# Order of casts, jobs and the last bank in a two-layer DiT kernel on one core

## The chip, the cores and the metric

The kernel runs on one core of one Trainium2 chip. Measured is the device time of one execution, in microseconds (us); lower is better. The engines are TensorE (PE, matrix products into PSUM banks of 512 columns), VectorE (DVE), ScalarE (ACT), GpSimd (POOL) and SyncE (SP), which here only issues DMAs; DMAs are also issued from POOL's and ACT's queues. Every engine works through its own queue in order.

## The reference

Two layers of a diffusion transformer over 256 tokens of width 2048, with 256 context tokens and a branch width of 4096, all in float32. Each layer computes

```python
h = _rmsnorm(x, g) * (1 + scale) + shift      # scale, shift, gate: silu(c) @ ada_w + ada_b
y = branch(h)                                 # layer 0: Fourier, layer 1: attention
x = x + gate * (y @ w_out)

def _fourier_branch(h, w_in, w_mix):
    u, z = jnp.split(h @ w_in, 2, axis=-1)
    ug = u.reshape(b, n, FNET_GROUPS, FNET_GROUP_DIM)
    f = jnp.fft.fft2(ug, axes=(1, 3), norm='ortho').real
    f = jnp.einsum('bngc,gcd->bngd', f, w_mix).reshape(b, n, D_BRANCH)
    return f * jax.nn.silu(z)
```

The branch of layer 1 is windowed attention with a sink and the context keys, gated by `silu(z)` too. At the end stands one more `_rmsnorm` with the gain `fg`, whose result is stored.

## The kernel before

All products are float32 in three passes: an operand is split into a high part `h`, its rounding to the matmul format (a cast on ACT, L62), and a low part `l`, what is left (a subtraction on DVE, L63), and `mm3` (L74) sends the three products h·h, h·l and l·h into one PSUM bank. So every weight that arrives passes through ACT and DVE before PE can use it. Weights are loaded by SP into three rotating slots named `raw`; a load that reuses a slot waits until the split that reads it is done.

A tile framework allots buffers, puts in the semaphores and orders each engine's instructions by a cost model's due times; `tc.issue_after(x)` tells it to put what is issued inside behind `x` in the order, without a wait.

The stages, in order of time: the opening (to about 120 us); sixteen Fourier groups `g` (to about 325); the gate `z` of layer 0 in 32 blocks `b` of 48 matmuls (to about 677); the output projection of layer 0 in 32 steps `i` of 48 matmuls (to about 1031); the norm between the layers; keys, values and attention of layer 1 (to about 1690); its output projection with the final norm (to the end).

What the change touches:

- *Fourier group, L512 to 610.* The weights of a group come in two halves `kh`, each with two column sets whose sum (`p`) and difference (`m`) are wanted. `fold_uh` (L128) forms the difference `wm` on DVE (L130), and the sum of the first half on DVE too (L136); for the second half, an accumulating DMA on POOL's queue adds one set onto the other in HBM-to-slot direction (L139). `split_part` casts and subtracts (`wph`, `wpl`, `wmh`, `wml`). `load_m(g)` (L397 to 418) makes the group's mixing matrices: sums `mt` on DVE (L401, L402), their split `mh`, `ml`, matmuls, and from their banks `pqh` (ACT), `pql` (DVE) and `sp` (ACT L416, DVE L417). Before, the split of the second half's `p` is emitted ahead of `load_m(g)`:

```python
        elif g > 4:
            with tc.issue_after(evacs[g - 2][1]):
                f3 = [fold_uh(load_uh(g, kh), g, kh) for kh in range(2)]
            w = [split_uh(*f3[0]), {"m": split_part("m", f3[1][1])}]
            with after_evac(g - 1):
                w[1]["p"] = split_part("p", f3[1][0])
```

- *Matvec jobs.* `ada_jobs` (L624) multiplies the conditioning vectors `cb` into weights on DVE, 64 jobs of one 1 MB load (`in_adw`) each: jobs 0 to 31 and 40 to 55 have eight products (L639), jobs 32 to 39 and 56 to 63 four. `next(ada)` runs one job. The gate stage runs one per block from b=4; the output projection runs `ada_rate.get(i, 1)` in step `i` (L747).
- *Norm between the layers, L792 to 818.* `rsqrt` (L79) takes a power on POOL (L88) and one Newton step on DVE (L89 to L91). Its result `r4`, four columns, is split into `r4h` (L801) and `r4l`; eight matmuls (L815) spread it over the partitions into one bank, ACT copies that to `r_bc1` (L816), and the first activations of layer 1 are scaled by it (L851, L852).
- *The end, L1165 to 1243.* The last 512 output columns (`cb` = 3) of the two blocks of 128 tokens (`tb`) are summed over 32 steps `k`; those of `tb` = 1 from k = 20 on are `held`, twelve matmuls of 512 columns being the last four steps. `evac` multiplies a bank by the gate (L1172), adds the residual (L1173) and squares with a row sum (ACT, L1174); `finish(tb)` adds the row sums (L87), takes the root (L88 to L91), scales four column blocks on ACT and DVE, and stores each (L1214).

Of the kernel before, what the change touches and what calls it, by code (L numbers as in the profile page):

```python
# [16 lines left out]
P = 128  # L17
D = 2048
# [10 lines left out]
def tile_dit(ctx: ExitStack, tc: tile.TileContext, a: dict, out: bass.AP):  # L29
# [46 lines left out]
        PE.matmul(o, wh, xl, start=False, stop=False)  # L76
        return PE.matmul(o, wl, xh, start=False, stop=stop).ins  # L77

    def rsqrt(pool, src, w, tag, ahead=None):  # L79
        v = pool.tile([P, w], F32, tag=tag + "v", name=tag + "v")  # L80
        t = pool.tile([P, w], F32, tag=tag + "s", name=tag + "s")
        r = pool.tile([P, w], F32, tag=tag + "r", name=tag + "r")
        if ahead is None:
            V.tensor_scalar(v, src, 1.0 / D, EPS, op0=ALU.mult, op1=ALU.add)
        else:
            V.tensor_scalar(v, ahead, 1.0 / D, EPS, op0=ALU.mult, op1=ALU.add)
            V.scalar_tensor_tensor(v, src, 1.0 / D, v, op0=ALU.mult, op1=ALU.add).ins  # L87
        GP.tensor_tensor(r, v, mhalf[:, 0:w], op=ALU.pow)  # L88
        V.tensor_tensor(t, r, r, op=ALU.mult)  # L89
        V.scalar_tensor_tensor(t, t, -0.5, v, op0=ALU.mult, op1=ALU.mult)  # L90
        V.scalar_tensor_tensor(r, t, 1.5, r, op0=ALU.add, op1=ALU.mult)  # L91
        return r

# [67 lines left out]
    with tc.tile_pool(name="st", reuse_waits="tile", bufs=1, side="right") as st:  # L161
# [230 lines left out]

        ua = us.enter_context(tc.tile_pool(name="ua", reuse_waits="tile", bufs=2))

        def load_m(g):
# [12 lines left out]
            mm3(o[:, GD : 2 * GD], ch[:, 1, :], cl[:, 1, :], mh[:, 1, :], lr[:, 1, :], True, True)  # L408
            o2 = psum()
            PE.matmul(o2[0:96, 0:GD], ch[:, 3, 0:96], mh[:, 0, :], start=True, stop=False)  # L410
            PE.matmul(o2[0:96, 0:GD], ch[:, 3, 0:96], lr[:, 0, :], start=False, stop=True)
            pqh = ua.tile([P, 512], F32R, tag="pqh", name="pqh")
            pql = ua.tile([P, 512], F32R, tag="pql", name="pql")
            split(pqh, pql, o)
            sp = ua.tile([96, GD], F32R, tag="sp", name="sp")
            S.activation(sp, o2[0:96, 0:GD], AF.Copy, scale=mk[:, g : g + 1])  # L416
            V.scalar_tensor_tensor(sp[64:96, :], o2[64:96, 0:GD], mk[64:96, g : g + 1], sp[64:96, :].bitcast(F32), op0=ALU.mult, op1=ALU.subtract)  # L417
            return pqh, pql, sp

        for p in range(8, 12):  # L420
# [91 lines left out]
    for g in range(G):  # L512
        if g == 2:
            mix0 = ft_end[0]
        if g == 3:
            with tc.issue_after(f0_end[0]):
                f3 = [fold_uh(load_uh(g, kh), g, kh) for kh in range(2)]
            w = [split_uh(*f3[0]), {"m": split_part("m", f3[1][1])}]
            with tc.issue_after(ft_end[0]), tc.issue_after(ft_end[2]):
                w[1]["p"] = split_part("p", f3[1][0])  # L520
            mix1 = ft_end[0]
        elif g == 4:
            w = []
            for kh in range(2):
                with tc.issue_after((mix0, mix1)[kh]):
                    v, m = fold_uh(load_uh(g, kh), g, kh)
                    w.append({"m": split_part("m", m)})
                    with after_evac(g - 1) if kh else nullcontext():
                        w[kh]["p"] = split_part("p", v)
# [122 lines left out]
    with tc.tile_pool(name="yp", reuse_waits="tile", bufs=32) as ypool:  # L652
# [148 lines left out]
    V.tensor_copy(r4h, r4)  # L801
    V.tensor_tensor(r4l, r4, r4h.bitcast(F32), op=ALU.subtract)
    r_bc1 = act()
    with tc.issue_after(st_end[0]):
# [5 lines left out]
        for c, tb in ((0, 0), (0, 1), (1, 0), (1, 1), (2, 0)):  # L810
            x1_turn(tb, c)
    o = psum()
    for t in range(4):
        for i, rp in enumerate((r4h, r4l)):
            bc_end = PE.matmul(o[:, t * P : (t + 1) * P], rp[:, t : t + 1].broadcast_to([P, P]), identr, start=i == 0, stop=i == 1).ins  # L815
    S.copy(r_bc1, o)  # L816
    with tc.issue_after(bc_end):
        x1_turn(1, 2)
# [20 lines left out]
    with tc.tile_pool(name="h1", reuse_waits="tile", bufs=16) as h1p:  # L839
# [3 lines left out]
        with tc.tile_pool(name="kvp", reuse_waits="tile", bufs=2) as kvp:  # L843
            hc1 = []
            for k in range(KT):
# [2 lines left out]
                t = kvp.tile([P, 512], F32, tag="ht", name="ht")  # L848
                for s, h in ((0, hx), (1, hc)):
                    q = slice(s * N, (s + 1) * N)  # L850
                    V.scalar_tensor_tensor(t[:, q], x1[k][:, q], gs1[:, k, s : s + 1], r_bc1[:, q], op0=ALU.mult, op1=ALU.mult)  # L851
# [303 lines left out]
        with tc.tile_pool(name="fin", reuse_waits="tile", bufs=1) as fp:  # L1155
# [12 lines left out]
            def evac(tb, cb, o, c0=0, c1=512, col=None):  # L1168
# [3 lines left out]
                V.tensor_tensor(t, o[:, qx], gbc[:, q], op=ALU.mult)  # L1172
                V.tensor_tensor(x, x, t, op=ALU.add)  # L1173
                S.activation(t, x, AF.Square, accum_out=ss[:, col : col + 1])  # L1174
                if cb < 3:
                    GP.tensor_tensor(x, x, fg[:, q], op=ALU.mult)

# [18 lines left out]
                    evac(tb, 1 + c, o[tb][c])  # L1196
            o = [psum() for _ in range(2)]

            def step(k, tb, wh, wl, q=slice(0, 512)):
                mm3(o[tb][:, q], yh[k][:, tb * P : (tb + 1) * P], yh[k][:, N + tb * P : N + (tb + 1) * P], wh[:, q], wl[:, q], k == 0, k == NB - 1)  # L1200

            def finish(tb):
                s2 = fp.tile([P, 1], F32, tag="s2", name="s2", bufs=2)
                V.tensor_reduce(s2, ss[:, tb * 4 : tb * 4 + 3], axis=AX.X, op=ALU.add)
                r = rsqrt(fp, ss[:, tb * 4 + 3 : tb * 4 + 4], 1, f"f{tb}", s2)
                for c in (0, 3, 1, 2):
                    t = x2[tb][c]
                    if c == 3:
                        V.scalar_tensor_tensor(t, t, r, fg[:, c * 512 : (c + 1) * 512], op0=ALU.mult, op1=ALU.mult)
                    elif c == 2:  # L1210
                        V.tensor_scalar(t, t, r, None, op0=ALU.mult)
                    else:
                        S.activation(t, t, AF.Copy, scale=r)
                    (nc.scalar if tb and c == 1 else nc.sync).dma_start(out[tb * P : (tb + 1) * P, c * 512 : (c + 1) * 512], t)  # L1214

            held = []
            for kg in range(8):
# [128 lines left out]
```

## Time and profile before

| | us |
| --- | --- |
| three runs | 1856.7, 1855.9, 1852.46 (median 1855.9) |
| profiled execution, its own time | 1853.2 |
| its span in the trace | 1851.4 |
| PE busy | 1813.9 |
| DVE busy | 1390.3 |
| ACT busy | 956.9 |
| POOL busy | 172.6 |

The granted clock of TensorE in the profiled execution is 0.998 of full speed. In the rows of the profile, "A B ENGINE Lnn ..." stands for a start, a duration, an engine and a line of the kernel before; "out<-in" names the tiles, followed by the sizes (partitions x elements), and a bracket gives the idle time of the engine ahead of the instruction and what ended it. Matmuls are pipelined, so their durations overlap and the distance of starts is what one costs.

### The profile page before, as it was taken

Reading aid. Unit: us, or ns where it says so; the run is one execution under the profiler, and the core shown is the slowest. Engines: PE = TensorE matmul, PEld = TensorE weight load, DVE = VectorE, ACT = ScalarE, POOL = GpSimd, SP = SyncE. Lnnn points to the kernel's source line nnn. Section 1 sums busy time; section 2 is a strip of 40 time slices with the busy share of each in tenths; the row PEclk is TensorE's granted clock in tenths of the full one; section 3 lists DMA queues with packets and bytes.
Section 4 is the critical chain, followed back from the end, with each engine's and each line's share of the span. In section 5 each row is a group of like instructions: output and inputs, shape, how many; then the busy total and the mean of one; then the engine's idle time right before and its main releaser. Section 6 shows DMA issues by size and latency. Waiting matters only on the chain.

```text
span 1851.4 us, 26496 instructions
## 1 busy us (share of the span) xinstructions
PE 1813.9 (98%) x9905; PEld 1548.0 (84%) x9905; DVE 1390.3 (75%) x2773; ACT 956.9 (52%) x1660; POOL 172.6 (9%) x183
## 2 busy tenths in 40 slices
PE   6999999999999999999999999999999999999997
PEld 4689999888888888878888888888888888888886
DVE  5687889786868788578974836888878878887454
ACT  5444545532222242224322524888888888897343
POOL 0001112000000000000000001111220220300000
PEclk9999999999999999999999999999999999999999
DMA  9988889666656647654675324333333333444543
GB/s 394 418 309 223 234 226 257 230 224 228 233 202 250 229 167 273 239 216 158 227 283 211 114 91 152 123 135 129 123 116 135 132 119 137 160 138 182 183 180 137
DMA packets 74305, 366.37 MB, mean 198 GB/s; under 512 B 21121, under 2 KB 21265, under 8 KB 39105
## 3 DMA queue, kind: packets, MB, share of 16 engines
q1 hardware_dynamic: 50112, 326.67, 48.2%
q0 software_dynamic: 19920, 31.06, 6.6%
q10 hardware_dynamic: 4144, 6.95, 1.1%
q8 instruction: 78, 1.28, 0.3%
q14 instruction: 51, 0.41, 0.1%
HBM read 352.06 MB, written 12.59 MB: 197 GB/s over the span
## 4 chain that ended last, share of the span: by engine, by line
PE 85%; DMA 2%; DVE 2%; issue 2%; ACT 1%; POOL 0%; POOLq 0%; ACTq 0%; DVEq 0%
PE ps L75 22%; PE ps L76 22%; PE ps L77 22%; PE ps L1045 6%; PE ps L1047 3%; PE ps L1101 3%; PE ps L1116 2%; PE ps L1115 2%; PE ps L1081 2%; PE ps L1082 2%; DMA raw<-in_wu 1%; DMA raw<-in_adw 1%; PE ps L961 0%; DMA raw<-in_wo 0%; ACT wh L62 0%
## 5 line engine op out<-in xcount | busy, mean ns | idle before, releaser
L62 ACT CAST wh<-raw 128x1024 fp32r<-128x1024 f32 x333 | 349.5, 1051 | 541.9 <-PE ps L76 457.6
L63 DVE TENSOR_TENSOR wl<-raw,wh 128x1024 fp32r<-128x1024 f32 x333 | 421.2, 1267 | 231.7 <-ACT wh L62 228.5
L76 PE MATMUL ps<-act,wh 128*128 128x512 f32 x1024 | 398.4, 389 | 0.0
L75 PE MATMUL ps<-act,wh 128*128 128x512 f32 x1024 | 394.3, 389 | 1.2 <-ACT wh L62 1.2
L77 PE MATMUL ps<-act,wl 128*128 128x512 f32 x1024 | 392.8, 389 | 0.5 <-DVE wl L63 0.5
L75 PEld LDWEIGHTS ps<-act,wh 128*128 128x128 f32 x1024 | 192.3, 188 | 41.2 <-ACT wh L62 1.7
L77 PEld LDWEIGHTS ps<-act,wl 128*128 128x128 f32 x1024 | 192.3, 188 | 40.9 <-DVE wl L63 1.0
L76 PEld LDWEIGHTS ps<-act,wh 128*128 128x128 f32 x1024 | 192.3, 188 | 39.6
L639 DVE CUSTOM_DVE_ANT_0 raw<-raw,cb 128x512 f32<-128x512 f32 x256 | 172.4, 687 | 23.6 <-DMA raw<-in_adw 20.1
L1045 PE MATMUL ps<-h,wh 128*128 128x512 f32 x512 | 186.5, 399 | 0.0
L639 DVE CUSTOM_DVE_ANT_0 junk<-raw,cb 128x512 f32<-128x512 f32 x192 | 131.7, 686 | 24.2 <-DMA raw<-in_adw 13.1
L1047 PE MATMUL ps<-h,wl 128*128 128x256 f32 x512 | 138.3, 280 | 0.0
L76 PE MATMUL ps<-wl,h 128*128 128x512 f32 x320 | 125.4, 393 | 0.0
L77 PE MATMUL ps<-wh,h 128*128 128x512 f32 x320 | 124.3, 391 | 0.0
L75 PE MATMUL ps<-wh,h 128*128 128x512 f32 x320 | 123.7, 396 | 0.5 <-ACT h L852 0.5
L1045 PEld LDWEIGHTS ps<-h,wh 128*128 128x128 f32 x512 | 96.1, 188 | 18.4
L1083 DVE CUSTOM_DVE_ANT_0 ps<-ps,mask,nsink 128x512 f32<-128x512 f32 x128 | 92.1, 753 | 11.7 <-PE ps L1082 10.7
L1086 ACT ACTIVATE p<-ps,mx 128x512 f32<-128x512 f32 x128 | 87.3, 687 | 24.9 <-DVE mx L1083 24.3
L1047 PEld LDWEIGHTS ps<-h,wl 128*128 128x128 f32 x512 | 96.9, 189 | 1.4
L63 DVE TENSOR_TENSOR pl<-ps,ph 128x512 fp32r<-128x512 f32 x128 | 83.7, 684 | 9.9 <-ACT ph L62 9.1
L1091 ACT ACTIVATE p<-p,sm 128x512 f32<-128x512 f32 x128 | 85.4, 716 | 7.9 <-DVE sm L1089 7.9
L75 PE MATMUL ps<-act,wph 128*127 128x260 f32 x256 | 73.5, 287 | 1.1 <-DVE act L239 1.1
(329 smaller groups left out, 3572.0 us busy)
## 6 DMA issues: line engine op xcount, KB each, us to landing
raw<-in_wz SPq DMA_DIRECT2D x64, 1024.0 KB, 4.9
raw<-in_adw SPq DMA_DIRECT2D x64, 1024.0 KB, 4.9
raw<-in_awp SPq DMA_DIRECT2D x32, 1024.0 KB, 12.8
raw<-in_wo SPq DMA_DIRECT2D x32, 1024.0 KB, 6.3
raw<-in_wq SPq DMA_DIRECT2D x32, 1024.0 KB, 4.9
raw<-in_wu SPq DMA_DIRECT2D x32, 1016.0 KB, 7.9
raw<-in_wo1b SPq DMA_DIRECT2D x16, 1024.0 KB, 4.8
act<-in_xT POOLq DMA_DIRECT2D x32, 256.0 KB, 6.0
```

Of the source, the lines that this page charges most:

```text
L62: last_cast[0] = S.copy(h, src).ins
L63: last_sub[0] = V.tensor_tensor(l, src, h.bitcast(F32), op=ALU.subtract).ins
L75: PE.matmul(o, wh, xh, start=start, stop=False)
L76: PE.matmul(o, wh, xl, start=False, stop=False)
L77: return PE.matmul(o, wl, xh, start=False, stop=stop).ins
L639: V.tensor_tensor_reduce(junk if s == 0 and i < 3 else wf, wf, cb[:, s, kq * 512 : kq * 512 + 512], 1.0, 0.0, ALU.mult, ALU.add, acc[:, i, ...
L1045: PE.matmul(o[0], wh[:, q], hx1[k], start=k == 0, stop=k == KT - 1)
L1047: PE.matmul(o[0][:, 0:N], wl[:, q], hx1[k][:, 0:N], start=False, stop=False)
L1083: V.tensor_tensor_reduce(o, o, mask[:, tb, :], -0.125, nsink[:, i : i + 1], ALU.add, ALU.min, mx[:, tb : tb + 1])
L1086: S.activation(pt[:, tb, :], so[tb], AF.Exp, bias=mx[:, tb : tb + 1], scale=-1.0, accum_out=sm[:, tb : tb + 1])
L1091: S.activation(pt[:, tb, :], pt[:, tb, :], AF.Copy, scale=sm[:, tb : tb + 1])
L1101: PE.transpose(o[:, (kt * 2 + tb) * P : (kt * 2 + tb + 1) * P], pt[:, tb, c : c + P], ident)
```

## The change

Six edits, in the order of the kernel:

1. `rsqrt` can write its result a second time, into `high`; `r4h` is written so, ahead of `r4`, in place of the cast from `r4`.
2. In Fourier groups from 4 on, the split of the second half's `p` is emitted after `load_m(g)` and ordered behind its last instructions on ACT and DVE.
3. The 64 matvec jobs are dealt out in another way: two in the blocks b = 10, 17, 24 of the gate stage, and a new table for the output projection.
4. The eight spreading matmuls run over `r4h` for all four columns first, then over `r4l`.
5. The first scaling of layer 1 names the bank `r_ps` itself as its operand instead of the copy `r_bc1`.
6. At the end, the first 28 steps of the last bank are closed and evacuated without the square; the last four steps run in two new banks of 256 columns, each evacuated by itself. In `finish` the earlier row sums and the constant are added ahead on DVE, the last row sum on POOL; the stores go in the order `c` = 2 (first half), 0, 2 (second half), 3, 1.

```diff
@@ rsqrt
+        if high is not None:
+            V.scalar_tensor_tensor(high, t, 1.5, r, op0=ALU.add, op1=ALU.mult)
         V.scalar_tensor_tensor(r, t, 1.5, r, op0=ALU.add, op1=ALU.mult)
@@ load_m
-            S.activation(sp, o2[0:96, 0:GD], AF.Copy, scale=mk[:, g : g + 1])
-            V.scalar_tensor_tensor(sp[64:96, :], ...)
+            m_end[0] = S.activation(sp, o2[0:96, 0:GD], AF.Copy, scale=mk[:, g : g + 1]).ins
+            m_end[1] = V.scalar_tensor_tensor(sp[64:96, :], ...).ins
@@ for g in range(G)
             w = [split_uh(*f3[0]), {"m": split_part("m", f3[1][1])}]
-            with after_evac(g - 1):
-                w[1]["p"] = split_part("p", f3[1][0])
+            v = f3[1][0]
...
             pqh, pql, sp = load_m(g)
+        if g > 3:
+            with after_evac(g - 1), tc.issue_after(m_end[0]), tc.issue_after(m_end[1]):
+                w[1]["p"] = split_part("p", v)
@@ z_out
-                        next(ada)
+                        for _ in range(2 if b in (10, 17, 24) else 1):
+                            next(ada)
@@ output projection of layer 0
-        ada_rate = {2: 2, 5: 2, 8: 2, 11: 2, 15: 0, 16: 0, 19: 2, 22: 2, 25: 2, 28: 2, 30: 0, 31: 0}
+        ada_rate = {2: 2, 4: 2, 6: 2, 14: 0, 15: 0, 16: 0, 25: 2, 26: 2, 27: 2, 28: 2, 29: 0, 30: 0, 31: 0}
@@ norm between the layers
-    r4 = rsqrt(const, ssum[1], 4, "q", ssum[0])
-    V.tensor_copy(r4h, r4)
+    r4 = rsqrt(const, ssum[1], 4, "q", ssum[0], r4h)
...
-    for t in range(4):
-        for i, rp in enumerate((r4h, r4l)):
-            bc_end = PE.matmul(o[:, t * P : (t + 1) * P], rp[:, t : t + 1].broadcast_to([P, P]), identr, start=i == 0, stop=i == 1).ins
+    r_ps = o
+    for i, rp in enumerate((r4h, r4l)):
+        for t in range(4):
+            bc_end = PE.matmul(o[:, t * P : (t + 1) * P], rp[:, t : t + 1].broadcast_to([P, P]), identr, start=i == 0 and t == 0, stop=i == 1 and t == 3).ins
@@ first scaling of layer 1
-                    V.scalar_tensor_tensor(t[:, q], x1[k][:, q], gs1[:, k, s : s + 1], r_bc1[:, q], ...)
+                    V.scalar_tensor_tensor(t[:, q], x1[k][:, q], gs1[:, k, s : s + 1], (r_bc1 if k or s else r_ps)[:, q], ...)
@@ finish
-                V.tensor_reduce(s2, ss[:, tb * 4 : tb * 4 + 3], axis=AX.X, op=ALU.add)
-                r = rsqrt(fp, ss[:, tb * 4 + 3 : tb * 4 + 4], 1, f"f{tb}", s2)
-                for c in (0, 3, 1, 2):
+                n = 3 + tb
+                with tc.issue_after(sum_end[0]):
+                    V.tensor_reduce(s2, ss[:, tb * 4 : tb * 4 + n], axis=AX.X, op=ALU.add)
+                V.tensor_scalar(s2, s2, D * EPS, None, op0=ALU.add)
+                last = ss[:, tb * 4 + n : tb * 4 + n + 1]
+                GP.tensor_tensor(v, last, s2, op=ALU.add)
+                GP.tensor_tensor(r, v, mhalf[:, 0:1], op=ALU.pow)
+                V.tensor_tensor(t2, r, r, op=ALU.mult)
+                V.scalar_tensor_tensor(t2, t2, -0.5 * D**0.5, v, op0=ALU.mult, op1=ALU.mult)
+                V.scalar_tensor_tensor(r, t2, 1.5 * D**0.5, r, op0=ALU.add, op1=ALU.mult)
+                for c, c0, c1 in ((2, 0, 256), (0, 0, 512), (2, 256, 512), (3, 0, 512), (1, 0, 512)):
@@ last steps
-            for k, w in held:
-                step(k, 1, *w)
-            evac(1, 3, o[1])
+            for k, w in held[:-4]:
+                step(k, 1, *w, last=NB - 5)
+            evac(1, 3, o[1], square=False)
+            for h in range(2):
+                q = slice(h * 256, h * 256 + 256)
+                o[1] = psum()
+                for k, w in held[-4:]:
+                    step(k, 1, *w, q, NB - 4)
+                evac(1, 3, o[1], q.start, q.stop, 7 + h)
             finish(1)
```

More of the change, by code (lines that the diff above doesn't have):

```diff
@@ L77, in mm3, with rsqrt @@
         return PE.matmul(o, wl, xh, start=False, stop=stop).ins
-    def rsqrt(pool, src, w, tag, ahead=None):
+    def rsqrt(pool, src, w, tag, ahead=None, high=None):
         v = pool.tile([P, w], F32, tag=tag + "v", name=tag + "v")
@@ L393, in tile_dit @@
         ua = us.enter_context(tc.tile_pool(name="ua", reuse_waits="tile", bufs=2))
+        m_end = [None, None]
         def load_m(g):
@@ L527, in tile_dit @@
                     w.append({"m": split_part("m", m)})
-                    with after_evac(g - 1) if kh else nullcontext():
-                        w[kh]["p"] = split_part("p", v)
+                    if kh == 0:
+                        w[0]["p"] = split_part("p", v)
         elif g > 4:
@@ L850, in tile_dit @@
                     q = slice(s * N, (s + 1) * N)
-                    V.scalar_tensor_tensor(t[:, q], x1[k][:, q], gs1[:, k, s : s + 1], r_bc1[:, q], op0=ALU.mult, op1=ALU.mult)
+                    V.scalar_tensor_tensor(t[:, q], x1[k][:, q], gs1[:, k, s : s + 1], (r_bc1 if k or s else r_ps)[:, q], op0=ALU.mult, op1=ALU.mult)
                     a_ = S.activation(h[:, 0:N], t[:, q], AF.Identity, bias=sh1[:, k, s : s + 1]).ins
@@ L1166, in tile_dit, with evac @@
             ss = fp.tile([P, 9], F32, name="ss")
-            def evac(tb, cb, o, c0=0, c1=512, col=None):
+            sum_end = [None]
+            def evac(tb, cb, o, c0=0, c1=512, col=None, square=True):
                 col = tb * 4 + cb if col is None else col
@@ L1172, in evac @@
                 V.tensor_tensor(t, o[:, qx], gbc[:, q], op=ALU.mult)
-                V.tensor_tensor(x, x, t, op=ALU.add)
-                S.activation(t, x, AF.Square, accum_out=ss[:, col : col + 1])
+                sum_end[0] = V.tensor_tensor(x, x, t, op=ALU.add).ins
+                if square:
+                    S.activation(t, x, AF.Square, accum_out=ss[:, col : col + 1])
                 if cb < 3:
@@ L1197, in tile_dit, with step @@
             o = [psum() for _ in range(2)]
-            def step(k, tb, wh, wl, q=slice(0, 512)):
-                mm3(o[tb][:, q], yh[k][:, tb * P : (tb + 1) * P], yh[k][:, N + tb * P : N + (tb + 1) * P], wh[:, q], wl[:, q], k == 0, k == NB - 1)
+            def step(k, tb, wh, wl, q=slice(0, 512), first=0, last=NB - 1):
+                mm3(o[tb][:, q], yh[k][:, tb * P : (tb + 1) * P], yh[k][:, N + tb * P : N + (tb + 1) * P], wh[:, q], wl[:, q], k == first, k == last)
             def finish(tb):
-                s2 = fp.tile([P, 1], F32, tag="s2", name="s2", bufs=2)
-                V.tensor_reduce(s2, ss[:, tb * 4 : tb * 4 + 3], axis=AX.X, op=ALU.add)
-                r = rsqrt(fp, ss[:, tb * 4 + 3 : tb * 4 + 4], 1, f"f{tb}", s2)
-                for c in (0, 3, 1, 2):
-                    t = x2[tb][c]
+                s2, v, t2, r = (fp.tile([P, 1], F32, tag=n_, name=n_, bufs=2) for n_ in ("s2", "fv", "ft", "fr"))
+                n = 3 + tb
[9 more added lines that the diff above has]
+                for c, c0, c1 in ((2, 0, 256), (0, 0, 512), (2, 256, 512), (3, 0, 512), (1, 0, 512)):
+                    t = x2[tb][c][:, c0:c1]
+                    q = slice(c * 512 + c0, c * 512 + c1)
                     if c == 3:
-                        V.scalar_tensor_tensor(t, t, r, fg[:, c * 512 : (c + 1) * 512], op0=ALU.mult, op1=ALU.mult)
+                        V.scalar_tensor_tensor(t, t, r, fg[:, q], op0=ALU.mult, op1=ALU.mult)
                     elif c == 2:
@@ L1213, in finish @@
                         S.activation(t, t, AF.Copy, scale=r)
-                    (nc.scalar if tb and c == 1 else nc.sync).dma_start(out[tb * P : (tb + 1) * P, c * 512 : (c + 1) * 512], t)
+                    (nc.scalar if tb and c == 1 else nc.sync).dma_start(out[tb * P : (tb + 1) * P, q], t)
             held = []
```

2 lines of the change are left out of this document (1 added, 1 removed).

## The prediction

> **What bounds the kernel now.** I read the page's busy shares first, then the waits of TensorE by releaser, then the timeline around each wait that the change could touch.
>
> ```profile
> span 1851.4 us, 26496 instructions
> PE 1813.9 (98%) x9905; PEld 1548.0 (84%) x9905; DVE 1390.3 (75%) x2773; ACT 956.9 (52%) x1660; POOL 172.6 (9%) x183
> ```
>
> TensorE works for 1813.9 of 1851.4 us, so all idle time of PE together is 37.5 us. The change removes no matmul, so it can only win back some of that and shorten what follows the last matmul. The second view names the waits (columns: the waiting line and who released it; us in total, times, longest).
>
> ```profile
> PE ps L76 <- DVE ml L63: 2.4, 2, 2.2
> PE ps L75 <- ACT wh L62: 1.2, 1, 1.2
> PE ps L815 <- DVE r4h L801: 0.9, 1, 0.9
> ```
>
> These three are the ones that the edits stand next to: the Fourier groups (`ml`), one step of the output projection of layer 0 (`wh`), and the norm between the layers (`r4h`). Everything else that the edits can reach is the end after the last matmul. I go through them in this order.
>
> **Fourier groups.** Each group starts with `load_m`'s matmuls, whose first row has tile `mh,ch`.
>
> ```profile
> 163.23 0.28 PE L75 MATMUL ps<-mh,ch 128*128 128x256 f32 x1
> 177.67 0.27 PE L75 MATMUL ps<-mh,ch 128*128 128x256 f32 x1
> 194.52 0.27 PE L75 MATMUL ps<-mh,ch 128*128 128x256 f32 x1
> 159.90 1.48 POOL L139 DMA_DIRECT2D raw<-in_wu  x1 [11.90 <-DVE wm L130]
> 169.63 1.05 ACT L62 CAST wph<-raw 128x1016 fp32r<-128x1016 f32 x1 [5.83 <-DMA raw<-in_wu]
> 164.88 1.21 DVE L130 TENSOR_TENSOR wm<-raw 128x1016 f32<-128x1016 f32 x1
> 170.71 1.22 DVE L63 TENSOR_TENSOR wpl<-raw,wph 128x1016 fp32r<-128x1016 f32 x1 [4.62 <-ACT wph L62]
> 173.69 0.48 DVE L417 SCALAR_TENSOR_TENSOR sp<-ps,mk,sp 32x256 fp32r<-32x256 f32 x1
> 179.37 0.68 DVE L63 TENSOR_TENSOR ml<-mt,mh 128x512 fp32r<-128x512 f32 x1
> ```
>
> One group takes 177.67 − 163.23 = 14.44 us where nothing stalls; the next takes 194.52 − 177.67 = 16.85, so 2.4 us are lost in it, which agrees with the 2.4 of the wait for `ml`. Why `ml` is late is in the other rows. POOL issues the accumulating load at 159.90. ACT's cast `wph` needs it and starts at 169.63, after 5.83 us of idling; DVE idles 4.62 us behind the cast. The results of `load_m` (`pqh`, `sp` on ACT; `pql`, `sp` on DVE) stand behind that cast in both queues though they need nothing of it. So the fold of the next group and finally `ml` come at 179.37, when PE has already been asking for it for about 2.2 us.
>
> The change emits this split after `load_m` and orders it behind `m_end`. ACT then does `pqh` and `sp` while the load is in flight, and DVE, free at 164.88 + 1.21 = 166.1, goes on with the half fold (1.2), `pql` (0.7), `sp` (0.5), the fold `wm` (1.2), two `mt` (0.4 each), before it needs the cast. That is 4.4 us, to 170.5. The cast still starts at 169.63 and ends at 170.7; `wpl` and `wml` (1.2 each) bring DVE to 173.1, and `ml` (0.68) ends at 173.8. PE asks for it at 179.37 + 0.68 − 2.2 = 177.9, so it is some 4 us ahead, and a fold held up by its own load by up to that much still costs nothing. What is now later is the second half of `p`: `wpl` ends at up to 173.1 instead of 171.9. Its matmuls are the last quarter of the group that begins at 177.67, so it has over 10 us. Gain 2.4 (2.0 to 2.9).
>
> **Order of the matvec jobs.** The step of the output projection that lost time:
>
> ```profile
> 806.50 0.39 PE L76 MATMUL ps<-act,wh 128*128 128x512 f32 x1
> 806.73 0.39 PE L77 MATMUL ps<-act,wl 128*128 128x512 f32 x1
> 809.96 0.40 PE L75 MATMUL ps<-act,wh 128*128 128x512 f32 x1
> 799.01 1.22 DVE L63 TENSOR_TENSOR wl<-raw,wh 128x1024 fp32r<-128x1024 f32 x1
> 800.25 0.33 SPq L46 DMA_DIRECT2D raw<-in_wo  x1
> 807.26 1.99 ACT L62 CAST wh<-raw 128x1024 fp32r<-128x1024 f32 x2 [15.60 <-DMA raw<-in_wo]
> L639 DVE CUSTOM_DVE_ANT_0 raw<-raw,cb x256: 676/687/695, 371.0 to 985.5; 128x512 f32<-128x512 f32 x128
> raw<-in_adw SPq DMA_DIRECT2D x64, 1024.0 KB, 4.9
> raw<-in_wo SPq DMA_DIRECT2D x32, 1024.0 KB, 6.3
> 442.45 1.05 ACT L62 CAST wh<-raw 128x1024 fp32r<-128x1024 f32 x1 [3.90 <-PE ps L76]
> ```
>
> Undisturbed, matmuls start 806.73 − 806.50 = 0.23 us apart. From 806.73 to 809.96 lie 3.23 us for four of them, which take 0.92, so 2.3 are lost. The chain: at i=11 `ada_rate` puts two heavy jobs (eight products of 0.687 us, 5.5 us each) into one step. The step's second weight half gets its `wl` only at 799.01, behind five of those products; the load of the next weights reuses that slot and so leaves at 800.25, lands at 807.26, and PE is out of weights. In the new table i=7 to 13 have one job each; three heavy jobs have gone to the gate stage (b=10, 17, 24), the doubles at i=2, 4, 6 and 25 to 28 are light (four products, 2.75 us). Before i=12 DVE has one job (5.5 us) less ahead of it in that step, `wl` comes that much earlier and so does the load: 5.5 against a lateness of 2.3. Gain 2.3.
>
> What may come in its place. A gate step has 48 matmuls, at 0.23 us 11 us; DVE does two `wl` (2.4), one product with the gate (0.7, as 128x512 products take in the last fence) and one heavy job (5.5), 8.6 in all. A double makes it 14.1 and overruns the step by 3.1, caught up at 2.4 a step. Against that stands that the casts wait for PE to give up a weight buffer (3.90 us at 442.45), so a load may come about that much late, and a `wl` more, before PE sees it: cost 0 to 0.5 for each of three. Among the old doubles with two heavy jobs (i=2, 11, 19, 22) only one shows up in the waits. The four light doubles in a row at i=25 to 28 each ask of a slot: landing 4.9, own job 2.75, at worst the other job 2.75 and the two `wl` 2.4 in front, 12.8 against 11: 1.8 lost per step at the very worst, 7.2 over four, less the lead that the single jobs before them leave (one job and one landing fewer than the slot's step has room for, 11 − 4.9 − 2.75 = 3.4), so 3.8; at best 4.9 + 2.75 = 7.7, nothing lost. Cost taken 0, the lead being the likelier to do, range 0 to 3.8.
>
> **Norm between the layers.**
>
> ```profile
> 1033.72 0.16 DVE L91 SCALAR_TENSOR_TENSOR qr<-qs,qr 128x4 f32<-128x4 f32 x1
> 1033.92 0.17 DVE L801 CAST r4h<-qr 128x4 fp32r<-128x4 f32 x1
> 1034.23 0.30 PE L815 MATMUL ps<-act,r4h 128*128 128x128 f32 x1 [0.93 <-DVE r4h L801]
> 1035.43 0.58 ACT L816 COPY act<-ps 128x512 f32<-128x512 f32 x1 [1.29 <-PE ps L815]
> 1036.05 1.67 DVE L851 SCALAR_TENSOR_TENSOR ht<-act,gs 128x256 f32<-128x256 f32 x4 [1.77 <-ACT act L816]
> ```
>
> `r4h` is written in the place of 1033.72 instead of 1033.92, so PE starts 0.2 earlier. `r4l` keeps its time, 1034.12 + 0.16; the first matmul that needs it stands behind four on `r4h`, which start at 1034.03 and, at the 0.117 between narrow matmuls in the last fence, take till 1034.5: it is there. Gain 0.2. The first scaling (1036.05) would come 0.6 earlier if it read the bank beside ACT's copy. But in the built program it waits for that copy: both read one bank and are put one behind the other. So this edit is costed at 0 (−0.6 to +0.1). The Trainium skill, "PSUM — Partial Sum Buffer", section "PSUM bank collisions raise a hardware error ⚠️", speaks against it: two engines on one bank in the same partitions collide, two reads too, and a scheduler has to add a dependency. By that rule the edit gives 0, without it 0.6; no run so far shows which.
>
> **The end.**
>
> ```profile
> 1840.45 0.39 PE L77 MATMUL ps<-wh,ys 128*128 128x512 f32 x1
> 1840.88 0.69 DVE L1172 TENSOR_TENSOR act<-ps,gbc 128x512 f32<-128x512 f32 x1 [3.58 <-PE ps L77]
> 1842.33 0.63 ACT L1174 ACTIVATE act<-act 128x512 f32<-128x512 f32 x1 [4.78 <-DVE act L1173]
> 1843.08 0.16 DVE L87 SCALAR_TENSOR_TENSOR f1v<-ss,f1v 128x1 f32<-128x1 f32 x1 [0.79 <-ACT act L1174]
> 1843.32 0.55 POOL L88 TENSOR_TENSOR f1r<-f1v,mhalf 128x1 f32<-128x1 f32 x1 [7.78 <-DVE f1v L87]
> 1844.49 0.75 DVE L1209 SCALAR_TENSOR_TENSOR act<-act,f1r,fg 128x512 f32<-128x512 f32 x1
> 1845.15 0.48 DVE L1211 TENSOR_SCALAR act<-act,f1r 128x512 f32<-128x512 f32 x1
> 1845.23 1.30 SPq L1214 DMA_DIRECT2D out<-act  x3
> 161.50 0.41 DVE L603 TENSOR_TENSOR ft<-ps,gsb 128x256 f32<-128x256 f32 x1
> 255.80 0.28 PE L77 MATMUL ps<-act,wml 128*127 128x256 f32 x1
> 256.15 0.28 PE L77 MATMUL ps<-act,wml 128*127 128x256 f32 x1
> ```
>
> Matmuls: twelve of 512 columns at 0.23 (2.8 us) become 24 of 256 at (256.15 − 255.80)/3 = 0.117, 2.8 us: 0, at worst +0.1 for weights that load no faster than before. The sum of the first 28 steps is added beside them (two DVE steps, 1.4 us of 2.8), and so is the first bank's. On the path remains one bank of half the width: two DVE steps of 0.41 for 0.69 (−0.56), ACT's square shorter by about 0.2 of its 0.63. −0.76.
>
> The last sum moves from DVE (from 1843.08 to POOL's start at 1843.32, 0.24) to POOL, in front of the power. Its price there is not in the trace. The nearest row is that power, 0.55 for the same 128x1; below it nothing but a share of the hop. I take 0.45, so +0.2 (−0.1 to +0.4). [...]
>
> Stores: the first goes when ACT's scaling is done, 1845.23, 0.74 after the factor is used first (1844.49). In the new order the first is 256 columns of the DVE's scaling, some 0.28 of the 0.48 at 1845.15, so it leaves about 0.4 earlier. But four issues stand in SP's queue then instead of three, at (1.30/3) 0.43 each, the last behind `c=3`, about as late as before; and what is left, 1851.4 − 1845.23 = 6.2 us, is landing. So between −0.4 and +0.3; I take −0.15, as one of its two ends doesn't move. Sum of the end: 0 − 0.76 + 0.2 − 0.15 = −0.7 (−1.3 to +0.1).
>
> **The sum.** 2.4 + 2.3 + 0.2 + 0.7 = 5.6 us. The profiled execution took 1853.2 us, so it would take 1847.6. The three runs lie at 1852.46 to 1856.7 with a median of 1855.9; the middle of the four is (1853.2 + 1855.9)/2 = 1854.55, and 1854.55 − 5.6 = 1849.0 is the forecast. A difference of 0.2% (3.7 us) is about what a measurement of this kernel tells from none.
>
> **Rivals.**
> - *Stall put off, not removed.* The four light doubles at the end run out of their lead (2 to 3), or the second half of `p` is late, or the fold's own load holds `ml` (2.4). For it: the worst slot time, 12.8, exceeds the step. Against: the four jobs ahead of it are light, and the old light doubles show no wait. Gain 5.6 − 2.5 = 3.1, time 1851.4: no change that can be told. Chance 0.18.
> - *Gate stage becomes DVE's* (slower). In each of b=10, 17, 24 two heavy jobs in a step put the next `wl`, and the load that reuses its slot, behind 11 us of products. It decides once PE's lead is below the overrun of 3.1 and the landing does not overlap it; the price is then 3.1 and half a landing of 4.9, 5.6 each, 17 in all less the gain: +11, time 1866. For: the old i=11 did just this. Against: the 3.90 us for which the casts wait there, plus the weight halves already cast, and three of four such doubles cost nothing. Chance 0.07, and 0.03 more that something of the kind costs 10.
> - *The first scaling does read beside the copy.* Gain 6.2, time 1848.4. The wait in the built program speaks against it. Chance 0.05.
> - *The end gains nothing* (POOL's sum as dear as a power and small stores slower, +0.1 instead of −0.7): 4.8, time 1849.8; still the forecast's side. Chance 0.15.
> - *The forecast as summed*: 0.52.
>
> **The numbers.** The forecast, the third and the fourth rival are faster by over 0.2%: 0.72, less 0.03 for a spread of the runs that hides it; stall put off 0.18 and those 0.03 are no change, 0.21; slower 0.10. Low end: every term at its better end, 2.9 + 2.3 + 0.8 + 1.3 = 7.3, is 1847.3, and some 1.8 below for the spread of runs (4.2 from lowest to highest): 1845.5. High end: the stall put off at its dearest, 5.6 − 3.8 = 1.8 of gain, 1852.75, and 1.8 for the spread: 1854.5.
>
> **What would show it.** Right: no wait of PE for `ml`, nor for `wh` and `wl` of the layer-0 projection; `pqh` before `wph` on ACT; groups 14.5 us apart throughout; `r4h`'s wait 0.7; 2.2 us from the last matmul's evacuation to the sum shrunk to 1.4; a POOL sum of 0.3 to 0.5. Wrong: a new wait for `wl` or `wh` near 420 to 600 us or in i=25 to 29, a gain of the end under 0.3, or a first scaling that starts before ACT's copy is over.

## Result and the profile after

Five runs of the changed kernel lie at 1845.7 to 1846.4 us, median 1845.93; five runs of before at 1852.46 to 1856.7, median 1854.19. The ratio is 0.9957, with a 95% interval of 0.9944 to 0.9970. The forecast was 1849.0 in a range of 1845.5 to 1854.5: sign and range held, but the gain was 8.3 by medians where 5.6 was summed. The page of the changed kernel begins so:

```profile
span 1844.5 us, 26534 instructions
PE 1812.6 (98%) x9917; PEld 1548.5 (84%) x9917; DVE 1395.3 (76%) x2777; ACT 958.1 (52%) x1662; POOL 173.8 (9%) x185
```

Twelve more matmuls, no more PE time, 6.9 us less span. The profiled execution took 1846.4 where that of before took 1853.2, so the two traces hold 6.8 of the 8.3. In the waits of PE (us in total, times, longest) `ml`, `wh` and `wl` have no row any more, and two of the edited norm are left:

```profile
PE ps L822 <- DVE r4h L92: 0.7, 1, 0.7
PE ps L75 <- ACT h L859: 0.5, 1, 0.5
```

**Fourier groups.** The timeline of the changed kernel, first ACT, then DVE, at the place shown of before:

```profile
165.65 0.59 ACT L62 CAST pqh<-ps 128x512 fp32r<-128x512 f32 x1 [1.76 <-PE ps L77]
168.88 1.05 ACT L62 CAST wph<-raw 128x1016 fp32r<-128x1016 f32 x1 [2.28 <-issue]
```

```profile
165.50 1.22 DVE L138 TENSOR_TENSOR raw<-raw 128x1016 f32<-128x1016 f32 x1
166.64 0.69 DVE L63 TENSOR_TENSOR pql<-ps,pqh 128x512 fp32r<-128x512 f32 x1
167.36 0.48 DVE L421 SCALAR_TENSOR_TENSOR sp<-ps,mk,sp 32x256 fp32r<-32x256 f32 x1
169.97 1.22 DVE L63 TENSOR_TENSOR wpl<-raw,wph 128x1016 fp32r<-128x1016 f32 x1 [0.20 <-ACT wph L62]
171.10 1.21 DVE L63 TENSOR_TENSOR wml<-wm,wmh 128x1016 fp32r<-128x1016 f32 x1
172.23 0.69 DVE L63 TENSOR_TENSOR ml<-mt,mh 128x512 fp32r<-128x512 f32 x1
```

`pqh` is now ahead of `wph`, DVE works through the time in which it idled 4.62 us, and `ml` ends at 172.9 instead of 180.1. The prediction had 173.8.

**Norm.** The first scaling names the bank as its operand, and waits for ACT's copy of that bank nevertheless:

```profile
1029.78 0.59 ACT L823 COPY act<-ps 128x512 f32<-128x512 f32 x1 [1.07 <-PE ps L822]
1030.40 0.48 DVE L858 SCALAR_TENSOR_TENSOR ht<-act,gs,ps 128x256 f32<-128x256 f32 x1 [1.54 <-ACT act L823]
```

It starts 0.62 after the copy, as before (1035.43, 1036.05). This agrees with the Trainium skill, "PSUM — Partial Sum Buffer", section "PSUM bank collisions raise a hardware error ⚠️", by whose rule the edit was worth nothing.

**The end.**

```profile
1834.77 0.28 PE L77 MATMUL ps<-wh,ys 128*128 128x256 f32 x1
1835.08 0.43 DVE L1181 TENSOR_TENSOR act<-ps,gbc 128x256 f32<-128x256 f32 x1 [0.53 <-PE ps L77]
1836.00 0.42 ACT L1184 ACTIVATE act<-act 128x256 f32<-128x256 f32 x1 [0.90 <-DVE act L1182]
1836.33 0.19 ACT L1184 ACTIVATION_READ_ACCUMULATOR act<-act 128x1 f32 x1
1836.59 0.19 POOL L1219 TENSOR_TENSOR fv<-ss,s 128x1 f32<-128x1 f32 x1 [6.79 <-ACT act L1184]
1836.86 0.55 POOL L1220 TENSOR_TENSOR fr<-fv,mhalf 128x1 f32<-128x1 f32 x1
1838.03 0.62 DVE L1230 TENSOR_SCALAR act<-act,fr 128x256 f32<-128x256 f32 x2
1838.45 1.85 SPq L1233 DMA_DIRECT2D out<-act  x4
```

From the start of the last matmul to the end of the span pass 1844.5 − 1834.77 = 9.73 us, 10.95 before (1851.4 − 1840.45). 1.56 of them lie before ACT's read of its row sum (2.42 before), and 6.47 behind the first use of the factor (6.91 before). The last matmul is narrower now and starts later for the same work, so the fairer count is from DVE's first step behind it: 9.42 for 10.52 us (1835.08, 1840.88), 1.1 less. From the start of the sum on POOL to the power pass 0.27 us, where I took 0.45.

### The profile page after: what moved, and what is told of

Read it like the earlier page. It is cut to its first block, busy times and chain, and to the rows that moved or that the text cites. A ratio compares the mean times of both kernels' runs of the same rounds, so it can differ in the third digit from the quotient of the medians.

```text
span 1844.5 us, 26534 instructions
## 1 busy us (share of the span) xinstructions
PE 1812.6 (98%) x9917; PEld 1548.5 (84%) x9917; DVE 1395.3 (76%) x2777; ACT 958.1 (52%) x1662; POOL 173.8 (9%) x185
## 4 chain that ended last, share of the span: by engine, by line
PE 93%; DMA 3%; DVE 2%; ACT 1%; issue 1%; POOL 0%; POOLq 0%; SPq 0%; ACTq 0%; DVEq 0%
PE ps L75 24%; PE ps L76 24%; PE ps L77 24%; PE ps L1052 6%; PE ps L1054 3%; PE ps L1108 3%; DMA raw<-in_awp 2%; PE ps L1123 2%; PE ps L1122 2%; PE ps L1088 2%; PE ps L1089 2%; PE ps L213 1%; DMA raw<-in_wu 1%; PE ps L968 0%; DMA xn<-in_x 0%
```

## The experiments

The experiments were run in three series. All are compared with runs of the kernel before on the same chip. In the first series, the next four kernels, these had a median of 1854.13 us and a spread from 1850.8 to 1858.9.

**Edit 2 alone.** The diff is that of the Fourier groups, on the kernel before.

```diff
+        if g > 3:
+            with after_evac(g - 1), tc.issue_after(m_end[0]), tc.issue_after(m_end[1]):
+                w[1]["p"] = split_part("p", v)
```

> Only edit 2 (the split of the second half's p behind load_m) on the kernel before. Sum of parts: the waits for ml go and the span ends 2.4 to 3.1 us earlier, while the wait for wh and wl at i=12 (1.7) stays. Rival, the stall is only put off: under 1 us. Third theory, on the 1.4 us that the runs gained beyond the profiled executions: the runs of before spread over 4 us because one of the stalls differs from run to run, and the edit that removes it also removes the spread; if it is this one, its runs lie within 1 us of each other and the gain by medians is 3.5 to 4.5.

Median 1848.64 us (1847.06 to 1851.4), ratio 0.9974 [0.9962, 0.9985]: 4.8 us by the ratio, more than the 2.4 of the sum. The wait for `ml` is gone, and the wait at i=12 is there, smaller than the 1.24 and 0.53 of the profiled execution of before:

```profile
803.92 0.50 PE L75 MATMUL ps<-act,wh 128*128 128x512 f32 x1 [0.51 <-ACT wh L62]
805.17 0.50 PE L77 MATMUL ps<-act,wl 128*128 128x512 f32 x1 [0.52 <-DVE wl L63]
```

The runs still spread over 4.3 us, so the third theory does not hold in its simple form: not all of the spread goes with this stall.

**Edit 3 alone.**

```diff
-                        next(ada)
+                        for _ in range(2 if b in (10, 17, 24) else 1):
+                            next(ada)
...
+        ada_rate = {2: 2, 4: 2, 6: 2, 14: 0, 15: 0, 16: 0, 25: 2, 26: 2, 27: 2, 28: 2, 29: 0, 30: 0, 31: 0}
```

> Only edit 3 (the new deal of the matvec jobs) on the kernel before. Sum of parts: the wait at i=12 goes, the span ends 2.3 us earlier, the waits for ml (2.4) stay. Rival, the gate stage or the four light doubles stall: under 1 us, with a new wait for wh or wl. Third theory (spread): if the stall at i=12 is the one that differs from run to run, these runs lie within 1 us and the gain by medians is 3.5 to 4.5.

Median 1853.03 (1850.87 to 1859.66), ratio 1.0003 [0.9991, 1.0014]: no difference shown, where 2.3 us were summed. The interval reaches from 1.7 us faster to 2.6 us slower, so it excludes the 2.3 and not a smaller gain. The runs spread over 8.8 us, so the third theory fails for this stall as well. The trace has no wait for `wh` or `wl` and no new one, so the mechanism worked; the changed kernel with this edit undone, below, is a second measure of what it is worth.

**Edit 6 alone.** The diff is that of `finish` and the last steps.

> Only edit 6 (last four steps in two banks of 256 columns, sum on POOL, stores) on the kernel before. Sum of parts: 1.1 us from the start of the last matmul to the end as the trace of the changed kernel shows it (9.73 for 10.95, and 0.1 lost on PE), where the prediction had 0.7. Rival, the shorter end shows only in the trace: under 0.3. The spread of the runs stays at some 4 us.

Median 1852.36 (1849.65 to 1856.12), ratio 0.9990 [0.9981, 1.0000]: 1.9 us faster, give or take 1.8, in keeping with 1.1.

**Edits 1, 4 and 5 alone.**

> Edits 1, 4 and 5 (r4h ahead, order of the spreading matmuls, first scaling from the bank) on the kernel before. Sum of parts: 0.2 us, the wait for r4h falls from 0.9 to 0.7, and the first scaling still starts after ACT's copy is over. Rival, the scaling reads beside the copy: 0.8. Neither is told from none by the times; the trace decides. The spread of the runs stays at some 4 us.

Median 1853.76 (1851.99 to 1856.48), ratio 0.9995 [0.9986, 1.0005]: not told from none, as expected. The wait for `r4h` is 0.7.

These kernels give more than their times: with the first profiled execution, three of them are executions of the old Fourier order. The wait for `ml` in them, in the timeline of PE, for before, edit 3, edit 6 and edits 1, 4, 5 in this order:

```profile
180.11 0.38 PE L76 MATMUL ps<-ml,ch 128*128 128x256 f32 x1 [2.16 <-DVE ml L63]
```

```profile
180.76 0.56 PE L76 MATMUL ps<-ml,ch 128*128 128x256 f32 x1 [2.62 <-DVE ml L63]
```

```profile
179.08 0.39 PE L76 MATMUL ps<-ml,ch 128*128 128x256 f32 x1 [1.20 <-DVE ml L63]
```

```profile
181.54 0.58 PE L76 MATMUL ps<-ml,ch 128*128 128x256 f32 x1 [2.92 <-DVE ml L63]
```

The cast that stands behind the accumulating load started at 169.63 in the first of them, and in the other three as follows:

```profile
170.27 1.05 ACT L62 CAST wph<-raw 128x1016 fp32r<-128x1016 f32 x1 [6.28 <-DMA raw<-in_wu]
```

```profile
168.60 1.05 ACT L62 CAST wph<-raw 128x1016 fp32r<-128x1016 f32 x1 [4.87 <-DMA raw<-in_wu]
```

```profile
171.07 1.05 ACT L62 CAST wph<-raw 128x1016 fp32r<-128x1016 f32 x1 [6.37 <-issue]
```

From 168.60 to 171.07, 2.5 us, the cast comes later, and the matmul on `ml` comes 2.5 us later too (179.08, 181.54); PE waits only 1.7 us longer (1.20, 2.92), as it also arrives later. The lateness is handed on from the group before. The load ahead of this cast takes much the same in all four, 9.7 to 10.1 us from POOL's issue to the cast, but is issued between 158.92 and 161.18. The issue waits for DVE's `wm`, and DVE stands behind the same kind of cast one group earlier (150.30 to 152.57), whose own load took 10.4 to 12.3 us.

The wait is not the whole price. The first matmuls of this group and of the next, for edit 3 and for edits 1, 4 and 5:

```profile
177.86 0.28 PE L75 MATMUL ps<-mh,ch 128*128 128x256 f32 x1
196.67 0.28 PE L75 MATMUL ps<-mh,ch 128*128 128x256 f32 x1
```

```profile
178.23 0.39 PE L75 MATMUL ps<-mh,ch 128*128 128x256 f32 x1
197.37 0.28 PE L75 MATMUL ps<-mh,ch 128*128 128x256 f32 x1
```

The group takes 18.81 and 19.14 us here, 16.85 in the execution of before and 15.93 with edit 6, where an undisturbed one takes 14.44. So waits of 1.20, 2.16, 2.62 and 2.92 us cost 1.5, 2.4, 4.4 and 4.7: behind the two longest the granted clock of TensorE fell to half, as the last section shows. From the group that starts at 163 us to the last one, these four executions need 146.99 to 149.86 us and that of edit 2 alone 144.70 (163.30 to 308.00). So the old order costs 2.3 to 5.2 us there, 3.8 in the mean.

**The changed kernel again, and its old deal of jobs.** The second series had the changed kernel as a yardstick beside it, and one with edit 3 undone.

```diff
-        ada_rate = {2: 2, 4: 2, 6: 2, 14: 0, 15: 0, 16: 0, 25: 2, ...}
+        ada_rate = {2: 2, 5: 2, 8: 2, 11: 2, 15: 0, 16: 0, 19: 2, 22: 2, 25: 2, 28: 2, 30: 0, 31: 0}
```

> The changed kernel once more, on the chip on which the next three run, as their yardstick. If the width of its runs is a property of the kernel: 1845.5 to 1846.5 again, against 8 us for before. If it was the luck of one chip: a spread of 3 us or more.

> The changed kernel with the old deal of the matvec jobs. The stall at i=12 was 2.3 us in the profiled execution of before, 1.6 with edit 2 alone, 0.7 with edit 6 alone and absent with edits 1, 4 and 5 alone, so its size changes between executions. If it is the load's landing that makes it change: 0 to 2.5 us slower than the changed kernel, 1.2 in the median, and a spread of 2 us or more. If the stall was worth its 2.3 all the time: 2.3 slower with a spread as the changed kernel's.

The changed kernel: 1846.33 (1845.77 to 1848.08). With the old deal: 1846.67 (1845.72 to 1847.36), its fastest run as fast as the other's. The profiled execution of the latter shows a stall at i=12 and a span of 1845.4 against 1843.9; the medians differ by 0.3. So the double at i=11 costs between nothing and 2.3 us, by the execution, and 0.3 in these medians of five runs each. That the first spread of 0.7 us was a property of the kernel is not so: in the third series the changed kernel's runs went from 1845.77 to 1850.08.

**The sum on DVE.**

```diff
-                GP.tensor_tensor(v, last, s2, op=ALU.add)
+                V.tensor_tensor(v, last, s2, op=ALU.add)
```

> The changed kernel with the last sum on DVE instead of POOL. Before, from ACT's read of its row sum (1842.87) to the power (1843.32) were 0.45; after, with the sum on POOL, 0.53 (1836.33 to 1836.86). If these two rows tell it, this kernel is the same or 0.1 us faster, which only the trace can show. If the prediction's price held (0.2 for the sum on POOL), 0.2 faster. If the POOL's sum saves a hop, as the change would have it, 0.1 to 0.2 slower.

Median 1846.37 (1845.61 to 1849.51) against 1846.33. The trace decides:

```profile
1835.92 0.19 ACT L1184 ACTIVATION_READ_ACCUMULATOR act<-act 128x1 f32 x1
1836.13 0.16 DVE L1219 TENSOR_TENSOR fv<-ss,s 128x1 f32<-128x1 f32 x1 [0.32 <-ACT act L1184]
1836.37 0.55 POOL L1220 TENSOR_TENSOR fr<-fv,mhalf 128x1 f32<-128x1 f32 x1 [7.06 <-DVE fv L1219]
```

0.45 us from the read to the power, 0.53 with the sum on POOL: the move costs 0.08. An instruction of 0.19 on POOL, with the hop to it, takes a little longer than one of 0.16 on DVE with two hops. The power of 0.55, which I took as the nearest row, was a poor guide to it. The Trainium skill, "GPSIMD Engine Reference", section "3.1 Elementwise — side-by-side cycle accounting", has about 156 ns for the dispatch of an instruction in the column of DVE; POOL's has no figure, only that it takes two dispatch hops to DVE's one. The trace's 0.19 against 0.16 has POOL's instruction slower by 0.03, and so does not speak against that.

**The old order of the stores.**

```diff
-                for c, c0, c1 in ((2, 0, 256), (0, 0, 512), (2, 256, 512), (3, 0, 512), (1, 0, 512)):
+                for c, c0, c1 in ((0, 0, 512), (3, 0, 512), (1, 0, 512), (2, 0, 512)):
```

> The changed kernel with the old order and width of the stores (c = 0, 3, 1, 2, all of 512 columns). From the first use of the factor to the end of the span were 6.91 us before and 6.47 after. If the narrower first store makes that: 0.4 slower, 6.9 in the trace. If landing differs by itself between executions by that much: no change.

Median 1847.27 (1846.44 to 1849.86), 0.9 above the yardstick with overlapping runs. Its timeline:

```profile
span 1845.2 us, 26526 instructions
1838.32 1.33 ACT L1232 ACTIVATE act<-act,fr 128x512 f32<-128x512 f32 x2 [1.51 <-DVE fr L1223]
1839.07 1.31 SPq L1233 DMA_DIRECT2D out<-act  x3
```

6.88 us from the first use of the factor to the end, with the new order 6.47, and 6.91 before. The first store leaves 0.75 after the factor instead of 0.42. The difference is not the landing's own: from the first use of the factor to the end, all eight traces with the new stores have 6.37 to 6.49 us, all six with the old ones 6.84 to 6.91. So the new stores make 0.4 us. This run puts back order and width together, so it does not tell which of the two does it.

**The sum of the second half on DVE.** On the kernel before, order kept; the accumulating load is replaced by a DVE addition.

```diff
-        if kh == 0 and g > 2:
+        if g > 2:
             V.tensor_tensor(v[:, :, 0, :], v[:, :, 0, :], v[:, :, 1, :], op=ALU.add)
```

> The kernel before, its order of emission kept, with the sum of the second half of the Fourier weights formed by DVE (as that of the first half is) instead of by the accumulating load on POOL's queue. In four executions of the old order the cast wph at the head of ACT's queue started at 168.6, 169.6, 170.3 and 171.1 and PE then waited 1.2, 2.2, 2.7 and 3.1 for ml, one for one. If it is the landing of that load that the queue stands behind, PE no longer waits for ml there, the runs come to 1848 to 1850 as with edit 2 alone, less 1.2 us of DVE per group where DVE is short. If it is the order of the queue as such, whatever stands at its head, the wait stays at over 1 us.

Median 1849.36 (1848.37 to 1851.26), ratio 0.9979 [0.9970, 0.9988]. The wait for `ml` is gone although the order is the old one, and at the end of the last group a new wait stands:

```profile
PE ps L75 <- ACT mh L62: 1.3, 1, 1.3
```

So it was the load's landing behind which the queues stood. Taking the load away does nearly as much as passing it.

**Three heavy doubles in a row.**

```diff
-                        for _ in range(2 if b in (10, 17, 24) else 1):
+                        for _ in range(2 if b in (10, 11, 12) else 1):
```

> The changed kernel with its three heavy doubles of the gate stage in a row, b = 10, 11, 12 instead of 10, 17, 24. DVE then overruns by 3.1 us three times without a step to catch up, 9.3 in all. If PE's lead there is what the casts' waits for weight buffers showed, some 4 us and the halves already cast (5.4 each), a stall of 0 to 3 us with a wait for wl or wh near 430 to 470. If the lead is nil, as the slower rival had it, 9 us or more. If the lead covers it all: no difference to the changed kernel.

Median 1853.83 (1852.93 to 1856.43), 7.2 us above the yardstick of its series (1846.62). This lies between my bounds, and the test was not clean: the second vector `cb` is loaded after job 7, which falls into the doubles here, and DVE idles 4.33 us for it at 451.31. What follows is a stall of PE at the next weights:

```profile
470.75 0.50 PE L75 MATMUL ps<-act,wh 128*128 128x512 f32 x1 [3.37 <-ACT wh L62]
472.34 0.79 PE L77 MATMUL ps<-act,wl 128*128 128x512 f32 x1 [0.85 <-DVE wl L63]
```

The slower rival's mechanism exists, then; spread over b = 10, 17 and 24 it leaves no wait in the trace, presumably since each double finds its lead restored. How much lead there is was not measured.

**The scaling ahead of the copy.** On the changed kernel, with the sum on DVE.

```diff
-    S.copy(r_bc1, o)
...
-                    V.scalar_tensor_tensor(t[:, q], ..., (r_bc1 if k or s else r_ps)[:, q], ...)
+                    V.scalar_tensor_tensor(t[:, q], ..., (r_bc1 if k else r_ps)[:, q], ...)
+                    if k == 0 and s == 1:
+                        with tc.issue_after(a_end):
+                            S.copy(r_bc1, r_ps)
```

> The changed kernel with the first two scalings of layer 1 put ahead of ACT's copy of the same bank (the copy and the transposed stores behind the first activation), and the last sum on DVE. The trace of the changed kernel has the scaling start 0.62 after the copy (1029.78, 1030.40) and PE idle 0.5 before its first product. If the two readers of a bank are only put one behind the other, scaling first gives PE that 0.5; the sum on DVE gives 0.08: 0.5 to 0.6 faster, by the trace, and about as much by the medians. If the copy or the stores behind it are then late for the next product: 0 or slower.

> The changed kernel once more as the yardstick of this call: 1845.5 to 1846.5 in the median.

Medians 1846.05 (1845.0 to 1847.01) and 1846.62 (1845.77 to 1850.08): 0.6 in the expected direction, with overlapping runs. The timeline of the former:

```profile
1029.93 0.63 PE L822 MATMUL ps<-act,r4h 128*128 128x128 f32 x4 [0.73 <-DVE r4h L92]
1031.05 0.87 DVE L855 SCALAR_TENSOR_TENSOR ht<-act,gs,ps 128x256 f32<-128x256 f32 x2 [0.87 <-PE ps L822]
1032.13 0.50 PE L75 MATMUL ps<-wh,h 128*128 128x512 f32 x1
```

From the first spreading matmul to the first product of layer 1 pass 2.20 us, and PE no longer waits for `h`; in the changed kernel it was 2.87 (1028.60 to 1031.47). So 0.67 us are won there, in this trace. The profiled execution as a whole is slower than the yardstick's (spans 1845.2 and 1844.0), because a wait of 1.3 us for `ml` came up in a later Fourier group. DVE's rows ahead of it:

```profile
274.05 1.22 DVE L63 TENSOR_TENSOR wpl<-raw,wph 128x1016 fp32r<-128x1016 f32 x1 [2.33 <-ACT wph L62]
275.19 1.21 DVE L132 TENSOR_TENSOR wm<-raw 128x1016 f32<-128x1016 f32 x1
```

Edit 2 orders the split behind `load_m`, but not behind the next fold `wm`; in this group the fold, and with it `mt` and `ml`, still stands behind the split that waits for the late cast. As the faster version this kernel is likely, not shown by its times.

## Why the prediction was right, and where its sizes were off

**Fourier groups: right in mechanism, too small in size.** The step "gain 2.4 (2.0 to 2.9)" read the price of the stall from one execution. At the first place alone it was 1.5, 2.4, 4.4 and 4.7 us in four executions, because the load came between 0 and 2.5 us later and because the clock fell behind the longer waits; the prediction had neither. Edit 2 alone brought 4.8 us by the ratio (2.8 to 7.0), and the 3.8 of the four traces lies within that. That the untraced runs are like the traced ones is likely, since the edit touches nothing else, but not shown. The two figures of 2.4 that the prediction found in agreement are not the same time: the row of waits holds 2.16 in this group and 0.26 in the next, and the next lost 0.6 more (209.53 − 194.52 = 15.01), which the sum left out.

The 4 us of slack worked out for `ml` were 177.9 − 172.9 = 5.0 at this place in the changed kernel's trace. It is not as much everywhere: two later groups of that trace take 14.89 and 14.70 us, so the sign "groups 14.5 us apart throughout" was missed there, and the executions with three doubles in a row and with the scaling first had 0.8 and 1.3 us of this wait in later groups.

**Jobs: right in mechanism, too large in size.** The step "5.5 against a lateness of 2.3. Gain 2.3" took the dearest execution for all of them. The stall was 2.3 there, 1.6 with edit 2 alone, 0.8 with edit 6 alone, absent with edits 1, 4 and 5 alone, 1.5 in the changed kernel with the old deal and 1.3 with the sum of the second half on DVE, 1.25 in the mean of the six. Edit 3 alone made no difference that the runs show, and undone in the changed kernel it costs 0.3 in the median; neither excludes 1.25. This error and that of the Fourier groups have opposite signs, and both come from reading a price in one execution; that they partly cancel in the medians is luck.

**What may come in its place: right.** No wait for weights arose, neither in the gate stage nor behind the four light doubles. "Cost taken 0" held at both. One double was misread: that of i=6 is not light, as its second job is job 40, with eight products. No wait followed it either.

**Norm: right.** 0.2 for `r4h`; 0 for the scaling from the bank, for the reason given. Scaling first, which the change did not do, shows that the 0.6 were there to be had.

**The end: too small.** Predicted 0 − 0.76 + 0.2 − 0.15 = −0.7. By the trace, from DVE's first step behind the last matmul to ACT's read of the row sum −0.74 (1.99 to 1.25), the sum on POOL +0.08, the stores −0.44, together −1.1. The new matmuls cost nothing: the two traces lie 5.8 us apart ahead of them and 5.8 at that first step (1840.88, 1835.08). The mis-sized terms are the sum on POOL and, above all, the stores: I let the last issue decide, but the end came earlier with an earlier first issue, though SP's last issue ended 0.2 later behind the factor.

**The sum.** 5.6 was worked out for the profiled execution, which gained 6.8. Of the difference of 1.2, 0.7 lie in the Fourier groups (the last of them ends 3.1 us earlier, at 322.95 for 326.01, where I had 2.4: the shorter waits of 0.2 and 0.3 in later groups went too), 0.4 at the end and 0.1 elsewhere. Of the further 1.5 to the 8.3 of the medians, 1.0 is by how much the median of before lies above its profiled execution (1854.19, 1853.2), and 0.5 by how much the median of the changed kernel lies below its own (1845.93, 1846.4). The measured 1845.93 lies below 1847.3, the sum of all terms at their better ends; the range holds it only by the 1.8 that was added for the spread of the runs.

## What to carry to other kernels

A stall behind a transfer has no price, only a distribution: before it is put into a sum, look at how late that load is in several executions and at the granted clock behind the stall, and keep the range open on the side of the later landing. An instruction that waits for a slow load at the head of a queue stops everything behind it on that engine and on those that it feeds; move what is ready ahead of it first, and only then look for time elsewhere. Naming a PSUM bank instead of its copy as an operand brings nothing as long as the copy is first in order; put the reader on the critical path first.

## What the runs showed of the hardware

Behind a long enough idle time of TensorE its granted clock fell to half for about 3 us. The view of busy time by stretch (stretch; us; busy time of PE, PEld, DVE, ACT, POOL; granted clock; DMA share; GB/s) has, behind the wait for `ml` of 2.16 us before, of 2.62 us with edit 3 and of 2.92 us with edits 1, 4 and 5, in this order:

```profile
182.00:184.00 2.00, 2.00 (x19) 2.00 (x18) 1.34 (x2) 0.00 (x0) 0.00 (x0) 1.00 1.09 312
```

```profile
182.00:184.00 2.00, 2.00 (x11) 2.00 (x11) 1.99 (x3) 0.00 (x0) 0.44 (x1) 0.50 1.18 363
```

```profile
182.00:184.00 2.00, 2.00 (x11) 2.00 (x11) 2.00 (x4) 0.51 (x3) 0.54 (x1) 0.50 1.35 303
```

In the kernel with three doubles in a row, around and behind the stall of 3.37 us:

```profile
466.00:470.70 4.70, 1.38 (x7) 0.80 (x5) 4.63 (x16) 1.64 (x3) 0.00 (x0) 1.00 0.70 263
473.00:475.50 2.50, 2.50 (x8) 1.98 (x7) 2.46 (x8) 0.00 (x0) 0.00 (x0) 0.54 1.02 383
475.50:480.00 4.50, 4.50 (x22) 3.70 (x21) 3.67 (x11) 1.64 (x2) 0.00 (x0) 1.00 0.79 275
```

The clock fell behind idle times of 2.62, 2.92 and 3.37 us, in the last case only in a second wait of 0.85 us that came right behind, and stayed at 1.00 behind those of 1.20 and 2.16. The Trainium skill, "TensorE: Matmul & The Clock Gate", "Part 1: The HAM clock gate", has the clock drop after an idle window of about 3.4 us; in this kernel it fell behind shorter ones, and the measurement decides. Whether there is a fixed limit, and where between 2.16 and 2.62 us, no run here shows. So a longer stall can cost more than its length. With three doubles in a row, the seven matmuls from 472.34 to 475.42 take 3.1 us where 1.6 would do at 0.23 each, 1.5 us more; two of them:

```profile
473.36 0.63 PE L76 MATMUL ps<-act,wh 128*128 128x512 f32 x1
473.78 0.63 PE L77 MATMUL ps<-act,wl 128*128 128x512 f32 x1
```
